# A conv-mixer trunk layer on one core: the written order kept on every engine through the first loop, x normed as it lands, tiny loads on GpSimd's queue

## The chip, the core and the metric

The kernel runs on one core of a Trainium2 chip. Five engines work side by side, each on a queue of its own and in order: TensorE (PE; PEld is its weight load), VectorE (DVE), ScalarE (ACT), GpSimd (POOL) and SyncE (SP), which only issues DMA transfers here. They wait for each other by semaphores. The metric is the device time of one execution in microseconds (us); lower is better.

## The reference, cut to what matters

One layer is computed. c is the conditioning vector; x has 2048 rows of 1024 float32 numbers.

```
def short_conv_mixer(h, w_in, conv_w, conv_b, w_out):
    u, gc, gb, z = jnp.split(h @ w_in, 4, axis=-1)
    v = gc * u
    conv = ...   # causal, depthwise, width 3, over the sequence
    y = gb * (conv + conv_b) * jax.nn.silu(z)
    return y @ w_out

    shift, scale, gate = ada_modulation(c, ada_w, ada_b)   # silu(c) @ w + b, split in three
    h = rmsnorm(x) * (1.0 + scale) + shift
    x = x + gate * short_conv_mixer(h, ...)
    return rmsnorm(x, final_g)
```

## The kernel before, in words

The sequence is cut into two halves of 1024 rows and each half into two blocks of 512. The four quarters of w_in (8192 columns) are taken in pairs g of 2 x 128 columns. For each pair a 2x2 scheme of seven products (Strassen's, in Winograd's form) stands for the eight block products, so a pair needs seven calls of `product`, 12 matmuls each. Every operand is split into a high part, rounded by ScalarE (`nc.scalar.copy`), and a low part, subtracted by VectorE (`tensor_sub`); three passes low-high, high-high and high-low make one float32 product.

Until its end the first loop is another matter, and it is what is changed. It runs over the eight slices k of 128 features of x. In step k TensorE multiplies slice k of h with the early weights of six pairs: 18 matmuls (line L542 before, L590 after) into six banks `ps["A"]`. Between these matmuls it does the steps of small jobs, one step after each matmul: `turn_h0(k + 1)` transposes the next slice of the four normed tiles of x0 (L143), has ScalarE make h from it (`make_h`, L147), splits it into b, and splits the early weights we of that slice; `turn_h1` does the same for the second block from k = 4 on, two slices in a step; `turn_mod(k + 2)` finishes the modulation (shift and scale) of a slice by small matmuls (L195).

The modulation of two slices is summed mostly on VectorE: `sum_mod` adds the scaled tiles of ada_w into the tile `mod` (L184, six instructions, four for the first), which starts with ada_b in its first row. The rest of the sum is done by the matmuls of `turn_mod`, of which the last for each of shift and scale reads `mod`. After step 3 the six banks hold the product P1, which is kept by copies (L359), three on VectorE and three on ScalarE; step 4 goes on in the same banks.

The norm of x (`norm_x`) is a square with a sum on ScalarE (L110), two GpSimd instructions on one column for 1/sqrt (ms L116, rs L118) and a scaling on VectorE (L133). `make_conv` loads the conv parameters and transposes them on TensorE (L243) into cpar. `warm_up(n)` is n matmuls on ones whose result is not used.

After the loop the 32 pairs of products follow (L300). `prepare(n)` loads the weights of product n if they are not there and splits its operand w; it runs four products ahead. `make_t3` and `make_t4` (L556, L561) make sums of h that the first of these products need later.

Buffers come from pools: raw has four (512 KB, early weights, weights, and in before the scratch of the squares too), op has 33, w has 6, PSUM has 8 banks, of which six are the early ones. The order on each engine is chosen by a scheduler that works on the recorded instructions with their dependencies and the order of writing as priority; loads wait in SyncE's queue in their order, and each also for the semaphore of the load eight before it.

Of the kernel before, what the change touches and what calls it, by code (L numbers as in the profile page):

```python
# [8 lines left out]
F32 = mybir.dt.float32  # L9
# [4 lines left out]
P = 128  # L14
# [4 lines left out]
def trunk_kernel(ctx: ExitStack, tc: tile.TileContext, x, c, final_g, ada_w, ada_b,  # L19
# [20 lines left out]
    nc = tc.nc  # L40
    S, D = x.shape
    E = w_out.shape[0]
    CW = conv_w.shape[0]
# [23 lines left out]
    def raw(name="raw"):  # L67
        return rawp.tile([P, D], F32, name=name, tag="raw")
# [32 lines left out]
    def warm_up(ps, a, n):  # L101

        for _ in range(n):
            nc.tensor.matmul(ps[:, :a.shape[1]], lhsT=a[:, :P], rhs=a, start=True, stop=True)


    def square_sum(src, scratch):

# [12 lines left out]
    def load_x(ci):  # L121

        xs = []
        for t in range(ci * ST, (ci + 1) * ST):
            a = op("xn", F32)
            nc.sync.dma_start(a.rearrange("p h n -> p (h n)"), x[t * P:(t + 1) * P, :])
            xs.append(a)
        return xs

    def norm_x(a):  # L130

        scratch = raw("sq").rearrange("p (h n) -> p h n", h=2)
        nc.vector.tensor_scalar_mul(a, a, rstd(square_sum(a, scratch)))  # L133

    def turn_x(xns, k):
# [27 lines left out]
    def mod_start(k):  # L163

        m = sp.tile([P, 2, MC], F32, name="mod", tag="sp")
        nc.gpsimd.memset(m, 0.0)
        nc.sync.dma_start(m[0:1], ada_b.rearrange("(o t n) -> o t n", o=1, t=3)[:, 0:2, k * P:k * P + MC])
        return m

    def load_ada(k):  # L170

        tiles = []
        for r in range(0, KD, AR):
            a = op("ada", F32).rearrange("p r (t n) -> p r t n", t=2)
            for t in range(2):
                nc.sync.dma_start(a[:, :, t, :], ada_v[:, r:r + AR, t, k * P:k * P + MC])
            tiles.append(a)
        return tiles
# [52 lines left out]
    def make_conv():  # L231

        rs = []
        for h in range(E // D):
            r = op("conv", F32).rearrange("p h n -> p (h n)")
            cols = slice(h * D, (h + 1) * D)
            nc.sync.dma_start(r[0:CW, :], conv_w[:, cols])
            nc.sync.dma_start(r[CW:CW + 1, :], conv_b[cols].unsqueeze(0))
            rs.append(r)
        ps = bank()  # L240
        for j in range(NJ):
            i = j % KD
            nc.tensor.transpose(ps[:, j * (CW + 1):(j + 1) * (CW + 1)], rs[j // KD][:CW + 1, i * P:(i + 1) * P],  # L243
                                ident[:CW + 1, :CW + 1])
        nc.vector.tensor_copy(cpar.rearrange("p j w -> p (j w)"), ps[:, :NJ * (CW + 1)])
# [166 lines left out]
    EU = 3  # L412
# [4 lines left out]
    def load_early(k):  # L417
        r = raw()[:, :2 * EU * P]
        for i, q in enumerate((Z, GC)):
            nc.sync.dma_start(r[:, i * EU * P:(i + 1) * EU * P].rearrange("p (j n) -> p j n", j=EU),  # L420
                              w_view[:, k, q, 0:EU, :])
        return r
# [27 lines left out]
    def sum_mod(k):  # L450
        mod_sum(mods[k], ada[k][:ON_DVE.get(k, KD // AR - 1)])

    def turn_mod(k):
        k2 = k // 2 * 2
        yield from mod_turn(mods[k2], ada[k2][ON_DVE.get(k2, KD // AR - 1):], k)

    def turn_h0(k):

        tp = bank()
        for t in range(ST):  # L460
            turn_one(tp, x0, k, t)
            if t < ST - 1:
                yield
        if k % KH == 0:
            h0.extend(half_block())
        make_h(h0[k], tp, k)
        bops[1 if k < KH else 2].append(split_op(h0[k]))
        split_early(k)
        yield
# [20 lines left out]
    def run_all(job):  # L490
        for _ in job:
            pass

    warm_up(early[-1].ps["A"], ones, 28)
    x0 = load_x(0)
    make_conv()
    for k in range(0, KD, 2):
        mods[k] = mod_start(k)
    ada[0] = load_ada(0)
    for k in range(2):  # L500
        we[k] = load_early(k)
    ada[2] = load_ada(2)
    for k in range(2, 4):
        we[k] = load_early(k)
    for a in x0:
        norm_x(a)
    sum_mod(0)
    warm_up(early[-1].ps["A"], ones, 16)
    for k in range(2):
        run_all(turn_mod(k))  # L510
    run_all(turn_h0(0))
    warm_up(early[-1].ps["A"], ones, 8)
    sum_mod(2)
    x1 = None
    for k in range(KD):
        if k == 0:
            ada[4] = load_ada(4)
            x1 = load_x(1)
            we[4] = load_early(4)
        elif k == 1:  # L520
            we[5] = load_early(5)
            ada[6] = load_ada(6)
        elif k == 2:
            we[6] = load_early(6)
            we[7] = load_early(7)
        jobs = []
        if k + 1 < KD:
            jobs.append(turn_h0(k + 1))
        if k >= KH:
            jobs += [turn_h1(2 * (k - KH) + i) for i in range(2)]  # L530
        if k + 2 < KD:
            jobs.append(turn_mod(k + 2))
        b = bops[1 if k < KH else 2][k % KH]
        if k == 1:
            sum_mod(4)
        if k == 3:
            for a in x1:
                norm_x(a)
            sum_mod(6)
        for n, (i, m) in enumerate(PASSES):  # L540
            for e, pr in enumerate(early):
                nc.tensor.matmul(pr.ps["A"], lhsT=wk[k][i][:, e * P:(e + 1) * P], rhs=b[:, m],  # L542
                                 start=k == 0 and n == 0, stop=k % KH == KH - 1 and n == 2, skip_group_check=True)
                while jobs and next(jobs[0], StopIteration) is StopIteration:
                    jobs.pop(0)
        for j in jobs:
            run_all(j)
        if k == KH - 1:
            for e, pr in enumerate(early):
                pr.keep_p1(kept(e, "p1"), nc.scalar.copy if e % 2 else nc.vector.tensor_copy)  # L550
    for e, pr in enumerate(early):
        pr.take_c11(kept(e, "c11"))

    def make_t3():
        for k in range(KH):
# [72 lines left out]
            yield  # L628


    work = [(0, g + d, p) for g in range(0, 2 * EU, 2) for p in (6, 5, 7, 4, 3) for d in range(2)]
    work += [(0, g, p) for g in range(2 * EU, NG) for p in ORDER]
    work += [(1, g, p) for g in range(NG) for p in ORDER]
    pairs = {(0, pr.g): pr for pr in early}
    weights, ready = {}, {}
    AHEAD = 4

    def prepare(n):
        if n >= len(work):
            return  # L640
        hf, g, p = work[n]
        for d in (0, 1):
            i = (hf * NG + g + d)
            if i < 2 * NG and i not in weights:
                weights[i] = Weights(i % NG)
        ready[n] = weights[hf * NG + g].operand(p)

    def side():
        yield from make_second()
        yield from make_gate()  # L650

    jobs = []
    for n in range(AHEAD):
        prepare(n)
    make_t3()
    second = {}
# [124 lines left out]
```

## Time and profile before

| | us |
|---|---|
| median of 3 runs | 1658.1 (1656.35 to 1658.23) |
| the profiled execution | 1657.11 |
| its span in the trace | 1655.3 |
| TensorE busy in it | 1624.2 (98%) |
| VectorE busy | 1036.7 (63%) |
| ScalarE busy | 532.6 (32%) |
| GpSimd busy | 163.7 (10%) |

The profile is of one execution. Its span ends with the last instruction; the execution's own time is 1.8 us longer. Shares of busy time are means over stages that have different limits.

### The profile page before, as it was taken

What the parts mean: (1) busy time and instruction counts of PE and PEld (TensorE: products, weight loads), DVE (VectorE), ACT (ScalarE), POOL (GpSimd) and SP (SyncE); (2) the same over time, 40 slices, a digit from 0 to 9 for tenths busy, and PEclk for the clock granted to TensorE, in tenths of its full rate; (3) what the DMA queues carried; (4) which work ended last, traced back from release to release, by engine and by line L of the source; (5) the groups of instructions that cost most, each with busy time, mean ns of one, the idle gap of its engine ahead of it and who ended that gap; (6) DMA issues with size and microseconds to landing.
All of it is one profiled execution on the core that took longest, in us unless ns stands there. A gap on an engine that the chain in (4) does not pass through costs nothing.

```text
span 1655.3 us, 19334 instructions
## 1 busy us (share of the span) xinstructions
PE 1624.2 (98%) x7276; PEld 1341.6 (81%) x7276; DVE 1036.7 (63%) x1596; ACT 532.6 (32%) x889; POOL 163.7 (10%) x234
## 2 busy tenths in 40 slices
PE   6999999999999999999999999999999999999997
PEld 6778788888888878888888888888888888888886
DVE  3798776777878876666666666666666742223331
ACT  2563344444433333333333333333333520111110
POOL 2101111101111110000001000111000100000000
PEclk7999999999999999999999999999999999999999
DMA  7624324244535632932222222222224633333320
GB/s 231 202 76 121 108 90 140 87 156 166 189 96 181 203 108 76 365 94 77 64 64 64 66 79 73 71 64 70 66 84 118 216 114 102 102 102 102 102 89 26
DMA packets 213103, 190.58 MB, mean 115 GB/s; under 512 B 7425, under 2 KB 181513, under 8 KB 213010
## 3 DMA queue, kind: packets, MB, share of 16 engines
q1 hardware_dynamic: 213010, 189.35, 36.1%
q8 instruction: 57, 0.93, 0.2%
q14 instruction: 36, 0.29, 0.1%
HBM read 144.75 MB, written 44.56 MB: 114 GB/s over the span
## 4 chain that ended last, share of the span: by engine, by line
PE 71%; issue 18%; DVE 6%; DMA 3%; POOL 2%; SPq 0%; ACT 0%; POOLq 0%; DVEq 0%; ACTq 0%
PE ps L300 63%; PE ps L718 5%; DMA raw<-in_l_w_in_dram 2%; DVE w L151 1%; PE ps L542 1%; POOL rs L118 1%; DMA ada<-in_l_ada_w_dram 1%; PE ps L143 1%; DVE b L151 1%; POOL t L323 1%; POOL ms L116 0%; DVE gate_m L216 0%; DVE t L322 0%; DVE raw L282 0%; DVE s L285 0%
## 5 line engine op out<-in xcount | busy, mean ns | idle before, releaser
L300 PE MATMUL ps<-b,w 128*128 128x512 f32 x5232 | 1192.5, 390 | 5.9 <-DVE v L387 2.4
L300 PEld LDWEIGHTS ps<-b,w 128*128 128x128 f32 x5232 | 980.4, 188 | 211.1 <-DVE v L387 3.3
L150 ACT CAST w<-raw 128x512 fp32r<-128x512 f32 x244 | 151.6, 623 | 371.4 <-PE ps L300 289.6
L150 ACT CAST w<-s 128x512 fp32r<-128x512 f32 x192 | 118.5, 618 | 202.2 <-PE ps L300 178.1
L718 PE MATMUL ps<-wo,ye 128*128 128x512 f32 x768 | 180.5, 394 | 0.0
L718 PE MATMUL ps<-wo,yw 128*128 128x512 f32 x768 | 176.8, 389 | 0.0
L151 DVE TENSOR_TENSOR w<-s,w 128x512 fp32r<-128x512 f32 x192 | 131.7, 687 | 67.9 <-ACT w L150 67.5
L718 PEld LDWEIGHTS ps<-wo,ye 128*128 128x128 f32 x768 | 144.2, 188 | 33.8
L151 DVE TENSOR_TENSOR w<-raw,w 128x512 fp32r<-128x512 f32 x244 | 168.3, 690 | 4.8 <-ACT w L150 4.6
L718 PEld LDWEIGHTS ps<-wo,yw 128*128 128x128 f32 x768 | 144.1, 188 | 30.3
L731 DVE TENSOR_TENSOR a<-ps,gate 128x512 f32<-128x512 f32 x32 | 22.0, 691 | 192.3 <-PE ps L718 192.2
L322 DVE SCALAR_TENSOR_TENSOR t<-v,cpar,t 128x512 f32<-128x512 f32 x128 | 95.8, 749 | 39.1 <-ACT t L320 38.3
L110 ACT ACTIVATE sq<-xa 128x1024 f32<-128x1024 f32 x16 | 17.0, 1060 | 274.2 <-DVE xa L732 251.7
L318 POOL COPY v<-v 128x2 f32<-128x2 f32 x32 | 21.4, 667 | 648.6 <-DVE v L370 618.5
L324 DVE TENSOR_TENSOR t<-t,gb 128x512 f32<-128x512 f32 x64 | 44.3, 692 | 53.9 <-POOL t L323 53.9
L275 DVE TENSOR_TENSOR s<-raw 128x512 f32<-128x512 f32 x64 | 44.1, 689 | 48.0 <-DMA raw<-in_l_w_in_dram 47.9
L399 DVE TENSOR_TENSOR u<-ps,u 128x512 f32<-128x512 f32 x58 | 40.0, 689 | 40.0 <-PE ps L300 40.0
L359 ACT COPY u<-ps 128x512 f32<-128x512 f32 x58 | 34.0, 586 | 91.4 <-PE ps L300 85.8
L320 ACT ACTIVATE t<-v,cpar 128x512 f32<-128x512 f32 x64 | 52.0, 814 | 5.1 <-DVE v L406 4.7
L116 POOL TENSOR_SCALAR ms<-ss 128x1 f32<-128x1 f32 x32 | 11.8, 369 | 411.5 <-ACT sq L110 387.1
L323 POOL TENSOR_TENSOR t<-t,sz 128x512 f32<-128x512 f32 x29 | 40.2, 1387 | 114.4 <-DVE t L322 94.1
L542 PE MATMUL ps<-b,we 128*128 128x512 f32 x144 | 46.9, 448 | 4.4 <-ACT b L150 1.5
(95 smaller groups left out, 998.6 us busy)
## 6 DMA issues: line engine op xcount, KB each, us to landing
raw<-in_l_w_in_dram SPq DMA_DIRECT2D x128, 512.0 KB
y_d<-t SPq DMA_DIRECT2D x64, 256.0 KB
yr<-y_d SPq DMA_DIRECT2D x32, 512.0 KB
op_d<-b SPq DMA_DIRECT2D x28, 512.0 KB
b<-op_d SPq DMA_DIRECT2D x28, 512.0 KB
xn<-in_x_dram SPq DMA_DIRECT2D x16, 512.0 KB
ada<-in_l_ada_w_dram SPq DMA_DIRECT2D x32, 256.0 KB
raw<-in_l_w_out_dram SPq DMA_DIRECT2D x16, 512.0 KB
```

Of the source, the lines that this page charges most:

```text
L150: nc.scalar.copy(hi, src)
L151: eng.tensor_sub(lo, src, hi.bitcast(F32))
L275: nc.vector.tensor_add(d, a21, a22)
L300: nc.tensor.matmul(ps, lhsT=w[:, i, k * P:(k + 1) * P], rhs=b[k][:, m], start=first and k == 0 and n == 0, stop=k == KH - 1 and n == 2, sk ...
L320: nc.scalar.activation(t, v[:, 2:], AF.Identity, bias=cpar[:, j, 3:4], scale=cpar[:, j, 2:3])
L322: nc.vector.scalar_tensor_tensor(t, v[:, w:CH + w], cpar[:, j, w:w + 1], t, ALU.mult, ALU.add)
L323: nc.gpsimd.tensor_mul(t, t, self.sz[ci])
L324: nc.vector.tensor_mul(t, t, self.gb[ci])
L359: (eng or nc.scalar.copy)(a, self.ps["A"])
L399: nc.vector.tensor_add(self.u, ps, self.u)
L542: nc.tensor.matmul(pr.ps["A"], lhsT=wk[k][i][:, e * P:(e + 1) * P], rhs=b[:, m], start=k == 0 and n == 0, stop=k % KH == KH - 1 and n == 2 ...
L718: nc.tensor.matmul(ps, lhsT=a, rhs=b, start=j == 0 and n == 0, stop=j == NJ - 1 and n == 2)
```

## The change

Five things are done. A helper `in_order` ties every instruction that is recorded between `mark` and the end of the first loop to the one before it on the same engine, so that the scheduler keeps the written order there. The code of that part is written in another order to go with it: the norm of x0 and `make_conv` stand before the modulation; the first slice's transposes before its modulation's sums; `sum_mod(4)`, `norm_all(x1)` and `sum_mod(6)` are jobs that stand behind `turn_h0` in steps 1 and 3; the first two `prepare` stand in the last step; the number of warm-ups is 28, 12, 16 and 4 in place of 28, 16 and 8. The scratch of `norm_x` comes from the pool op in place of raw. The loads of ada_b (four) and of the conv parameters (four) are issued by GpSimd in place of SyncE. The loads of ada slice 4 and of the first weights are issued earlier in the code.

```
+    def in_order(mark):
+
+        last = {}
+        for i in nc.cur_bb.bb.instructions[mark:]:
+            if i.engine in last:
+                tc.add_manual_dep(i, last[i.engine].name, mybir.DependencyInfo(
+                    mybir.DependencyClass.NoSync, mybir.DependencyReason.DATA), reason="in_order")
+            last[i.engine] = i
...
-        scratch = raw("sq").rearrange("p (h n) -> p h n", h=2)
+        scratch = op("sq", F32)
...
-        nc.sync.dma_start(m[0:1], ada_b.rearrange("(o t n) -> o t n", o=1, t=3)[:, 0:2, k * P:k * P + MC])
+        nc.gpsimd.dma_start(m[0:1], ada_b.rearrange("(o t n) -> o t n", o=1, t=3)[:, 0:2, k * P:k * P + MC])
...
-            nc.sync.dma_start(r[0:CW, :], conv_w[:, cols])
-            nc.sync.dma_start(r[CW:CW + 1, :], conv_b[cols].unsqueeze(0))
+            nc.gpsimd.dma_start(r[0:CW, :], conv_w[:, cols])
+            nc.gpsimd.dma_start(r[CW:CW + 1, :], conv_b[cols].unsqueeze(0))
...
+    def load_weights(i):
+        if i < 2 * NG and i not in weights:
+            weights[i] = Weights(i % NG)
...
+    def now(f, *args):
+
+        f(*args)
+        return
+        yield
+
+    def norm_all(xs):
+        for a in xs:
+            norm_x(a)
+
+    mark = len(nc.cur_bb.bb.instructions)
     warm_up(early[-1].ps["A"], ones, 28)
     x0 = load_x(0)
+    begin()
+    norm_all(x0)
     make_conv()
...
-    for a in x0:
-        norm_x(a)
+    warm_up(early[-1].ps["A"], ones, 12)
+    first = turn_h0(0)
+    for _ in range(ST - 1):
+        next(first)
     sum_mod(0)
     warm_up(early[-1].ps["A"], ones, 16)
-    for k in range(2):
-        run_all(turn_mod(k))
-    run_all(turn_h0(0))
-    warm_up(early[-1].ps["A"], ones, 8)
+    run_all(turn_mod(0))
+    run_all(first)
+    warm_up(early[-1].ps["A"], ones, 4)
+    run_all(turn_mod(1))
     sum_mod(2)
...
+            jobs.append(now(sum_mod, 4))
...
+        elif k == 3:
+            load_weights(0)
+            jobs += [now(norm_all, x1), now(sum_mod, 6)]
+        elif k == 5:
+            load_weights(1)
         if k >= KH:
             jobs += [turn_h1(2 * (k - KH) + i) for i in range(2)]
+        if k == KD - 1:
+            jobs += [now(prepare, 0), now(prepare, 1)]
...
-        if k == 1:
-            sum_mod(4)
-        if k == 3:
-            for a in x1:
-                norm_x(a)
-            sum_mod(6)
...
         pr.take_c11(kept(e, "c11"))
+    in_order(mark)
...
-    for n in range(AHEAD):
+    for n in range(2, AHEAD):
         prepare(n)
```

`begin` holds the loads that stood between `make_conv` and the norm of x0 before, and those of ada slice 4. How the rows move shows at three places. Line numbers are 9 higher in the new kernel at first, 48 higher in the loop.

The first is the start of the program. On TensorE it began so, L243 being the transposes of the conv parameters and L195 `turn_mod`:

```order
L104 MATMUL ps<-ones 128x128 x44
L243 MATMUL ps<-ident,conv 128x4 x8
L104 MATMUL ps<-ones 128x128 x8
L243 MATMUL ps<-ident,conv 128x4 x8
L195 MATMUL ps<-sc,ada 128x1 x6
L195 MATMUL ps<-ones,mod 128x1
L195 MATMUL ps<-sc,ada 128x1 x4
L195 MATMUL ps<-ones,mod 128x1
```

It now begins with fewer warm-ups, then all conv transposes, and three transposes of x (L152) stand between the warm-ups that follow:

```order
L104 MATMUL ps<-ones 128x128 x28
L252 MATMUL ps<-ident,conv 128x4 x16
L104 MATMUL ps<-ones 128x128 x12
L152 MATMUL ps<-ident,xn 128x128 x3
L104 MATMUL ps<-ones 128x128 x16
L204 MATMUL ps<-sc,ada 128x1 x4
L204 MATMUL ps<-ones,mod 128x1
L204 MATMUL ps<-sc,ada 128x1 x4
L204 MATMUL ps<-ones,mod 128x1
```

The loads that those conv transposes wait for are now on GpSimd, where they stand behind the last of the four norms of x0 (ms and rs of its fourth tile are the first two rows):

```order
L125 TENSOR_SCALAR ms<-ss 128x1
L127 TENSOR_TENSOR rs<-ms,nhalf 128x1
L246 DMA conv<-in_l_conv_w_dram 3x1024
L247 DMA conv<-in_l_conv_b_dram 1x16x64
L246 DMA conv<-in_l_conv_w_dram 3x1024
L247 DMA conv<-in_l_conv_b_dram 1x16x64
```

In before they were the first loads of SyncE's queue behind the four of x.

The second place is the end of step 3 on VectorE, where the norm of x1 (xn), the sums of the last modulation (mod) and the copies of P1 (keep) stand. Before, the scheduler had mixed them among the splits b and we:

```order
L151 TENSOR_TENSOR b<-hr,b 128x512 x2
L184 SCALAR_TENSOR_TENSOR mod<-ada,sc,mod 128x512
L133 TENSOR_SCALAR xn<-xn,rs 128x1024
L184 SCALAR_TENSOR_TENSOR mod<-ada,sc,mod 128x512
L133 TENSOR_SCALAR xn<-xn,rs 128x1024
L151 TENSOR_TENSOR b<-hr,b 128x512
L133 TENSOR_SCALAR xn<-xn,rs 128x1024
L151 TENSOR_TENSOR we<-raw,we 128x768
L133 TENSOR_SCALAR xn<-xn,rs 128x1024
L359 COPY keep<-ps 128x512 x3
L151 TENSOR_TENSOR we<-raw,we 128x768
```

Now all of the norm and of the sums stands ahead of the copies, and the splits of steps 3 and 4 around them:

```order
L160 TENSOR_TENSOR b<-hr,b 128x512
L160 TENSOR_TENSOR we<-raw,we 128x768
L142 TENSOR_SCALAR xn<-xn,rs 128x1024 x4
L193 SCALAR_TENSOR_TENSOR mod<-ada,sc,mod 128x512 x6
L368 COPY keep<-ps 128x512 x3
L160 TENSOR_TENSOR b<-hr,b 128x512
L160 TENSOR_TENSOR we<-raw,we 128x768
```

The third place is the end of the loop on VectorE. The names t hold the last four sums of the second block, s the sums of the first weights, w the operands of the first products. Before, the operands w were split among the last sums:

```order
L151 TENSOR_TENSOR b<-hr,b 128x512
L151 TENSOR_TENSOR w<-s_836,w 128x512
L486 TENSOR_TENSOR t_737<-hr 128x512
L151 TENSOR_TENSOR w<-s_823,w 128x512
L486 TENSOR_TENSOR t_752<-hr 128x512
L151 TENSOR_TENSOR b<-t_737,b 128x512
L151 TENSOR_TENSOR w<-s_834,w 128x512
L151 TENSOR_TENSOR b<-t_752,b 128x512
L486 TENSOR_TENSOR t_773<-hr 128x512
L556 TENSOR_TENSOR hr<-hr 128x512
L486 TENSOR_TENSOR t_788<-hr 128x512
L151 TENSOR_TENSOR b<-t_773,b 128x512
```

Now the last sum with all that is made from it stands first (L605 and L610 are `make_t3` and `make_t4`), and the first operand w behind it:

```order
L495 TENSOR_TENSOR t_804<-hr 128x512
L605 TENSOR_TENSOR hr<-hr 128x512
L610 TENSOR_TENSOR hr<-hr,t_804 128x512
L160 TENSOR_TENSOR b<-t_804,b 128x512
L284 TENSOR_TENSOR s_811<-raw 128x512
L288 TENSOR_TENSOR s_813<-s_811,raw 128x512
L291 TENSOR_TENSOR raw<-raw 128x512
L160 TENSOR_TENSOR w<-s_813,w 128x512
```

## Rows read from the trace of the kernel before

**Rows 1.** page, busy time of TensorE, share of the span, instructions

```profile
PE 1624.2 (98%) x7276; PEld 1341.6 (81%) x7276; DVE 1036.7 (63%) x1596; ACT 532.6 (32%) x889; POOL 163.7 (10%) x234
```

**Rows 2.** TensorE grouped by line, 92 us to the end; idle before them

```profile
L300 PE MATMUL ps<-b,w 128*128 128x512 f32 x5232 | 1192.5, 390 | 5.9 <-DVE v L387 2.4 <-ACT w L150 1.7 <-DVE gb L385 1.7
```

**Rows 3.** timeline of TensorE, 0 to 135 us (start, length; idle before in brackets)

```profile
15.27 0.66 PE L243 MATMUL ps<-ident,conv 4*128 4x4 f32 x8
17.24 1.02 PE L195 MATMUL ps<-sc,ada 128*128 128x1 f32 x8 [1.31 <-DMA ada<-in_l_ada_w_dram]
18.63 1.01 PE L195 MATMUL ps<-sc,ada 128*128 128x1 f32 x4 [0.37 <-DMA ada<-in_l_ada_w_dram]
...
38.32 0.79 PE L542 MATMUL ps<-b,we 128*128 128x512 f32 x1 [1.52 <-ACT b L150]
```

**Rows 4.** timeline of ScalarE, 0 to 110 us

```profile
2.37 0.21 ACT L81 ACTIVATE sc<-c_sb 128x8 f32<-128x8 f32 x1 [0.36 <-DMA c_sb<-in_c_dram]
...
27.63 1.06 ACT L110 ACTIVATE sq<-xn 128x1024 f32<-128x1024 f32 x1 [0.29 <-DVE we L151]
...
57.85 1.06 ACT L110 ACTIVATE sq<-xn 128x1024 f32<-128x1024 f32 x1 [3.22 <-issue]
```

**Rows 5.** timeline of SyncE's queue (length is the issue, not the transfer)

```profile
0.72 0.39 SPq L79 DMA_DIRECT2D c_sb<-in_c_dram  x1
...
3.96 0.26 SPq L237 DMA_DIRECT2D conv<-in_l_conv_w_dram  x1
...
5.10 4.84 SPq L167 DMA_DIRECT2D mod<-in_l_ada_b_dram  x4
9.99 4.98 SPq L176 DMA_DIRECT2D ada<-in_l_ada_w_dram  x8
```

**Rows 6.** timeline of GpSimd, 0 to 100 us

```profile
1.66 1.45 POOL L166 MEMSET mod<- 128x512 f32 x3
28.87 0.34 POOL L116 TENSOR_SCALAR ms<-ss 128x1 f32<-128x1 f32 x1 [25.75 <-ACT sq L110]
...
32.45 1.32 POOL L118 TENSOR_TENSOR rs<-ms,nhalf 128x1 f32<-128x1 f32 x1
...
34.56 0.93 POOL L118 TENSOR_TENSOR rs<-ms,nhalf 128x1 f32<-128x1 f32 x1
```

**Rows 7.** windows: busy us by engine, granted clock, DMA share, GB/s

```profile
0.00:8.00 8.00, 6.96 (x47) 6.96 (x48) 0.65 (x4) 1.49 (x2) 2.55 (x10) 1.00 0.72 259
...
18.00:19.00 1.00, 0.63 (x5) 0.55 (x4) 0.96 (x2) 0.00 (x0) 0.00 (x0) 0.59 1.11 365
...
42.00:43.00 1.00, 1.00 (x7) 0.92 (x8) 0.82 (x2) 0.65 (x2) 0.00 (x0) 0.97 0.87 262
```

**Rows 8.** ScalarE, then VectorE: timeline rows of the operations of a loop step

```profile
36.84 0.78 ACT L147 ACTIVATE hr<-ps,shift,scale 128x512 f32<-128x512 f32 x1 [4.22 <-PE ps L143]
37.65 0.62 ACT L150 CAST b<-hr 128x512 fp32r<-128x512 f32 x1
...
42.41 0.83 ACT L150 CAST we<-raw 128x768 fp32r<-128x768 f32 x1 [0.35 <-DMA ada<-in_l_ada_w_dram]
...
28.38 4.68 DVE L184 SCALAR_TENSOR_TENSOR mod<-ada,sc,mod 128x512 f32<-128x512 f32 x6
...
35.52 0.75 DVE L133 TENSOR_SCALAR xn<-xn,rs 128x1024 f32<-128x1024 f32 x1 [0.46 <-POOL rs L118]
36.18 0.95 DVE L151 TENSOR_TENSOR we<-raw,we 128x768 fp32r<-128x768 f32 x1
38.30 0.69 DVE L151 TENSOR_TENSOR b<-hr,b 128x512 fp32r<-128x512 f32 x1 [1.16 <-ACT b L150]
...
67.20 1.88 DVE L359 COPY keep<-ps 128x512 f32<-128x512 f32 x3
```

**Rows 9.** timeline of TensorE again: step k = 4, and the first main product

```profile
67.94 0.50 PE L542 MATMUL ps<-b,we 128*128 128x512 f32 x1 [1.37 <-DVE keep L359]
...
92.18 16.48 PE L300 MATMUL ps<-b,w 128*128 128x512 f32 x72
```

More of the change, by code (lines that the diff above doesn't have):

```diff
@@ L492, in run_all, with prepare, begin @@
             pass
+    work = [(0, g + d, p) for g in range(0, 2 * EU, 2) for p in (6, 5, 7, 4, 3) for d in range(2)]
+    work += [(0, g, p) for g in range(2 * EU, NG) for p in ORDER]
+    work += [(1, g, p) for g in range(NG) for p in ORDER]
+    pairs = {(0, pr.g): pr for pr in early}
+    weights, ready = {}, {}
+    AHEAD = 4
+    def load_weights(i):
+        if i < 2 * NG and i not in weights:
+            weights[i] = Weights(i % NG)
+    def prepare(n):
+        if n >= len(work):
+            return
+        hf, g, p = work[n]
+        for d in (0, 1):
+            load_weights(hf * NG + g + d)
+        ready[n] = weights[hf * NG + g].operand(p)
+    def begin():
+        for k in range(0, KD, 2):
+            mods[k] = mod_start(k)
+        ada[0] = load_ada(0)
+        for k in range(2):
+            we[k] = load_early(k)
+        ada[2] = load_ada(2)
+        for k in range(2, 4):
+            we[k] = load_early(k)
+        ada[4] = load_ada(4)
+    def now(f, *args):
+        f(*args)
+        return
+        yield
[3 more added lines that the diff above has]
+    mark = len(nc.cur_bb.bb.instructions)
     warm_up(early[-1].ps["A"], ones, 28)
     x0 = load_x(0)
+    begin()
+    norm_all(x0)
     make_conv()
-    for k in range(0, KD, 2):
-        mods[k] = mod_start(k)
-    ada[0] = load_ada(0)
-    for k in range(2):
[L501 to L504, printed above, removed]
-    for a in x0:
-        norm_x(a)
+    warm_up(early[-1].ps["A"], ones, 12)
+    first = turn_h0(0)
+    for _ in range(ST - 1):
+        next(first)
     sum_mod(0)
     warm_up(early[-1].ps["A"], ones, 16)
-    for k in range(2):
-        run_all(turn_mod(k))
-    run_all(turn_h0(0))
-    warm_up(early[-1].ps["A"], ones, 8)
+    run_all(turn_mod(0))
+    run_all(first)
+    warm_up(early[-1].ps["A"], ones, 4)
+    run_all(turn_mod(1))
     sum_mod(2)
-    x1 = None
     for k in range(KD):
+        jobs = []
+        if k + 1 < KD:
+            jobs.append(turn_h0(k + 1))
         if k == 0:
-            ada[4] = load_ada(4)
             x1 = load_x(1)
@@ L525, in trunk_kernel @@
             we[7] = load_early(7)
-        jobs = []
-        if k + 1 < KD:
-            jobs.append(turn_h0(k + 1))
+        elif k == 3:
[3 more added lines that the diff above has]
+            load_weights(1)
         if k >= KH:
             jobs += [turn_h1(2 * (k - KH) + i) for i in range(2)]
+        if k == KD - 1:
+            jobs += [now(prepare, 0), now(prepare, 1)]
         if k + 2 < KD:
@@ L628, in begin_out @@
             yield
[L631 to L646, printed above, removed]
     def side():
```

## The prediction

> **What bounds the kernel now.** I read the summary page first. TensorE is busy 98% of the span [rows 1], so a change can win only where TensorE stands still, or where something pushes that standing still further out. The grouping of TensorE's instructions from 92 us to the end leaves 5.9 us of idle time in front of all 5,232 main products [rows 2]. Everything else that can be won lies in the first 92 us, the part that this change reorders. Both ends of that part stand in the TensorE timeline: the first loop matmul starts at 38.32 [rows 3], step k = 4 at 67.94 and the first main product at 92.18 [rows 9]. From there on TensorE runs almost without a gap, so a microsecond by which the first main product moves is about a microsecond of the result.
>
> Why is the first matmul so late? On ScalarE the first square of x waits for VectorE's split of an early weight and starts at 27.63 [rows 4], because the scratch of the squares is a buffer of the four-deep raw ring, which the early weights hold. Yet the first tile of x had landed by 5.10: there SyncE's next load, which waits for its semaphore, goes out [rows 5].
>
> The sum runs against the profiled execution's own 1657.1 us, 1.8 us over its span and 1.0 us below the median of the runs. I take 0.2% (3.3 us) as the least that a measurement of this kernel tells from no change.
>
> **Part 1, the start.** With scratch of its own, the norm of x0 follows the loads. GpSimd, though, now issues eight DMAs, and the four conv loads stand behind its last rstd. Three memsets end at 3.11 today [rows 6]; the four modulation loads between them add 4d, where d is one issue on GpSimd, which no row shows. The nearest rows: SyncE issues such a load in as little as 0.26 [rows 5]; GpSimd needs 0.93 to 1.32 for a power on one column, which is all overhead [rows 6]. I take 1.0, since it is software on that engine, and keep 0.26 and 1.3 as ends. The first square can reach GpSimd at 5.10 + 1.24 (27.63 to 28.87 [rows 4, 6]) = 6.3, so with d = 1.0 the memsets and issues end later, at 7.1. The four ms/rs pairs took 28.87 to 35.49, 6.6 us [rows 6]: 13.7. The last conv load is issued 3 d later, at 16.7. Its landing: 1.65 us on an empty queue (c_sb, issue at 0.72, used at 2.37 [rows 4, 5]); about 4.1 us behind bulk loads (the last of the eight ada issues, near 14.5, is used at 18.6 [rows 3, 5]). The queue is full here, so I take the middle, 2.9: the conv tables are in at 19.6.
>
> On this point the Trainium skill speaks against the change: "DMA: Bandwidth & Descriptors", section "Anatomy of one DMA — SWDGE (gpsimd) path", gives a DMA issued from GpSimd a fixed cost of about 2.0 us. By that figure, as an estimate, the landing would come 0.9 us sooner and the sum below would be 0.9 us smaller; no run here shows it yet.
>
> What stands behind them on TensorE, in order: the conv transposes (0.66 [rows 3]), 12 warm-ups, three transposes of x, 16 warm-ups, turn_mod(0). TensorE has then been idle since about 9 us. The granted clock fell to half (0.59 in that slice) about 2.7 us after the last dense work at 15.9 [rows 3, 7], so these 28 warm-ups start at 1.2 GHz. At the program's start 47 records, two a warm-up, took from 1.04 to 8.0 [rows 7], so 28 take about 8.0. The transposes take 0.5. Turn_mod(0) has 20 records at 1.02 / 8 [rows 3]: 2.5. Then the shift and last transpose 0.5, ScalarE's make_h 0.78, cast of b 0.62, cast of we 0.83, VectorE's we 0.95 [rows 8]: 3.7. Sum 15.4; first loop matmul at 19.6 + 15.4 = 35.0, against 38.3: **−3.3 us**. With the low ends (d 0.26, landing 1.65) it is 30.8, −7.5; with the high ones (1.3, 4.1) 38.3, no gain.
>
> SyncE's queue gets shorter and the bulk loads land some 3 us earlier. I price that at nothing: in the new order the loop waits for VectorE and TensorE, and the loads are hidden behind them.
>
> **Part 2, steps k = 0 to 3.** A step without waits is 24.24 / 4 = 6.1 (67.94 to 92.18 [rows 9]). In k = 0, turn_mod(2) ends in a matmul on mod[2], whose six sums now stand behind the split of we[0]: 4.68 [rows 8], while TensorE gets there after 7 of 18 matmuls, 2.4: a wait of 2.3.
>
> In k = 3 norm_all and sum_mod(6) are queued on VectorE ahead of the three copies that keep P1, and step 4's first matmul overwrites the bank of the first copy. From the step's first matmul: four matmuls with the transposes 1.4; make_h, b, we 2.23 [rows 8]; first square to GpSimd 1.24; four ms/rs pairs 6.6; the last xn 0.75; six sums 4.68; one copy 0.63 (three in 1.88 [rows 8]). Sum 17.6, of which TensorE has work for 6.1. Today the same squares start at 57.85 [rows 4] in the scheduler's order, ten microseconds ahead of step 4, and the copies cost only 1.37 [rows 9]. In the new order nothing covers the chain. Steps 0 to 3 take 3 × 6.1 + 2.3 + 17.6 = 38.2, against 29.6 (38.32 to 67.94): **+8.6 us**.
>
> **Part 3, k = 4 to the first main product.** ScalarE serves in order, and each h1 tile now holds it for make_h 0.78, VectorE's subtraction 0.69 and its cast 0.62. A step costs ScalarE 2.23 + 2 × 2.09 = 6.4. From 1.4 after the start, three steps and step 7's two tiles: 1.4 + 19.2 + 4.2 = 24.8. Then VectorE, in the written order: two subtractions and a b (2.1), S1 and S2 (1.4), ScalarE's cast 0.62, the split of w 0.69: 29.6, and about 0.9 because VectorE has four operations a tile (2.8) against the 2.09. So 30.5 against 24.24: **+6.3 us**, most of it a gap of some 6 us ahead of the first product, where prepare(0) now stands last.
>
> **Part 4, what follows gaps.** After two such gaps (11 and 6 us) I expect half clock, as after 15.9. The loop's first matmul took 0.79 and the full clock came back by 42.1 [rows 3, 7], 3.7 us after 38.3, so each costs up to 1.8: **+3 us**, as part of it lies in waits (ends 0 and 3.7). In the main loop the second operand is split about 1 us late, and of the 5.9 us of idle [rows 2] about half should vanish, as VectorE stands further ahead of TensorE when that starts: **−2 us** (ends −5 and +1).
>
> Sum: −3.3 + 8.6 + 6.3 + 3 − 2 = +12.6; 1657.1 + 12.6 = 1669.7 us.
>
> **Rivals.**
> - *Even.* The order holds, but every open price falls on its good end: conv in early (−7.5 for −3.3), no drop of the clock (0 for 3), the idle time back (−5 for −2): 12.6 − 4.2 − 3 − 3 = +2.4, 1659.5. For it: GpSimd has nothing else to do there. Against it: three independent goods at once.
> - *Faster.* The start decides: if GpSimd hands its loads to the queue without holding them behind its own work, conv lands with the last tile of x, near 9.4 (the fourth modulation load, which waits for that tile, is out at 9.94 [rows 5]). The first matmul would then stand at 9.4 + 15.4 = 24.8, a gain of 13.5; with 8.6 + 6.3 against it and part 4 at its best end, −5, the sum is −3.6: 1653.5. It decides once that first matmul comes before about 25. Against it: the conv loads stand behind four rs, which themselves wait for the last tile of x.
> - *Much slower.* Each issue costs GpSimd 2 us or more, or both turn_mods run at half clock (2.5 more for each): the first matmul at 40 to 45, the sum 1675 to 1680. For it: GpSimd's rows are long. Against it: a cheap SyncE issue.
>
> **How the numbers follow.** Forecast 62%, even 14%, faster 9%, much slower 15%. The range 1657 to 1680 leaves out the faster case and the upper half of the last, under 2 in 10. Slower by over 0.2%: 0.62 + 0.15 = 0.77; within: 0.14; faster: 0.09.
>
> **What the new profile would show.** Right: conv transposes near 19 to 20, first loop matmul near 35, a TensorE gap of about 11 us before step 4 that ends with VectorE's copy, a second gap of about 6 us before the first main product, the first product near 104. Wrong: a first matmul before 25; the squares of x1 well before step 3's copies are due; or products that follow the loop without a gap. If the gaps are there and the time is not, the 5.9 us of later idle came back in full.

## The result and the profile after

The changed kernel takes 1675.8 us in the median (1671.7 to 1681.1, 4 runs) against 1658.2 (1656.4 to 1664.0, 4 runs) for the kernel before on the same chip: a ratio of 1.0106, 95% interval 1.009 to 1.0122. The profiled execution took 1675.6 us with a span of 1673.8, so 18.5 us of span were added.

TensorE's instructions grouped by line and tile (busy us, mean ns of one, idle us in front of them with what ended it) answer to [rows 2]:

```profile
L309 PE MATMUL ps<-b,w 128*128 128x512 f32 x5232 | 1197.1, 391 | 11.7 <-DVE w L160 6.9 <-DVE v L396 2.7 <-DVE gb L394 1.2
...
L590 PE MATMUL ps<-b,we 128*128 128x512 f32 x144 | 53.6, 487 | 10.6 <-DVE keep L368 10.4 <-DVE we L160 0.2
...
L252 PE MATMUL ps<-ident,conv 4*128 4x4 f32 x16 | 2.0, 242 | 8.5 <-DMA conv<-in_l_conv_b_dram 8.5
```

Three waits stand out: 8.5 us for the conv tables, 10.4 for a copy of P1, and 6.5 of the 6.9 in front of the first main product. The start, on GpSimd's timeline and then on TensorE's:

```profile
11.47 0.57 POOL L127 TENSOR_TENSOR rs<-ms,nhalf 128x1 f32<-128x1 f32 x1
11.99 0.93 POOL L246 DMA_DIRECT2D conv<-in_l_conv_w_dram  x1
12.92 0.53 POOL L247 DMA_DIRECT2D conv<-in_l_conv_b_dram  x1
...
13.94 0.51 POOL L247 DMA_DIRECT2D conv<-in_l_conv_b_dram  x1
```

```profile
18.25 0.98 PE L252 MATMUL ps<-ident,conv 4*128 4x4 f32 x8 [7.91 <-DMA conv<-in_l_conv_b_dram]
19.85 0.98 PE L252 MATMUL ps<-ident,conv 4*128 4x4 f32 x8 [0.61 <-DMA conv<-in_l_conv_b_dram]
20.76 4.46 PE L104 MATMUL ps<-ones 128*128 128x128 f32 x24
...
34.76 0.79 PE L590 MATMUL ps<-b,we 128*128 128x512 f32 x1 [0.23 <-DVE we L160]
```

x is normed with the loads (the last rs at 11.47), the tables' last load goes out at 13.94 and is used at 19.85, and the first loop matmul stands at 34.76 instead of 38.32 [rows 3]. VectorE's timeline ahead of step 4 and ahead of the first main product:

```profile
67.87 0.75 DVE L142 TENSOR_SCALAR xn<-xn,rs 128x1024 f32<-128x1024 f32 x1 [0.76 <-POOL rs L127]
68.54 4.68 DVE L193 SCALAR_TENSOR_TENSOR mod<-ada,sc,mod 128x512 f32<-128x512 f32 x6
73.14 1.88 DVE L368 COPY keep<-ps 128x512 f32<-128x512 f32 x3
...
103.90 0.68 DVE L160 TENSOR_TENSOR b<-t,b 128x512 fp32r<-128x512 f32 x1
...
106.59 0.69 DVE L160 TENSOR_TENSOR w<-s,w 128x512 fp32r<-128x512 f32 x1
```

And TensorE's main products up to the first transposes of x's second half (243.66 us; before, these stood at 225.12):

```profile
107.34 19.11 PE L309 MATMUL ps<-b,w 128*128 128x512 f32 x72 [6.48 <-DVE w L160]
126.84 27.53 PE L309 MATMUL ps<-b,w 128*128 128x512 f32 x120 [0.39 <-DVE w L160]
156.40 29.10 PE L309 MATMUL ps<-b,w 128*128 128x512 f32 x120 [2.03 <-DVE v L396]
186.21 57.61 PE L309 MATMUL ps<-b,w 128*128 128x512 f32 x252 [0.71 <-DVE v L396]
```

The first 72 records took 19.11 us, not 16.48 [rows 9], and the granted clock is what differs: 0.50 from 108 to 112 us. In the view by windows the columns are the stretch, its length, busy us (and records) of TensorE, its weight loads, VectorE, ScalarE and GpSimd, then the granted clock, the DMA share and GB/s:

```profile
18.00:22.00 4.00, 3.13 (x22) 3.09 (x23) 1.10 (x3) 0.00 (x0) 0.00 (x0) 0.50 1.10 348
...
34.00:36.00 2.00, 1.77 (x8) 1.33 (x9) 1.96 (x3) 0.23 (x2) 0.00 (x0) 0.55 0.93 355
...
42.00:45.00 3.00, 3.00 (x10) 2.32 (x9) 0.00 (x0) 0.00 (x0) 0.00 (x0) 0.59 0.81 226
...
74.00:78.00 4.00, 4.00 (x13) 2.91 (x13) 1.02 (x2) 1.00 (x2) 0.00 (x0) 0.50 0.00 0
...
108.00:112.00 4.00, 4.00 (x11) 3.13 (x10) 3.08 (x5) 2.88 (x6) 0.00 (x0) 0.50 0.46 131
...
156.00:160.00 4.00, 3.60 (x10) 2.86 (x11) 4.00 (x8) 1.09 (x2) 0.00 (x0) 0.64 0.02 8
```

The 18.5 us add up: first loop matmul 34.76 − 38.32 = −3.6; steps 0 to 3, 39.2 against 29.6, +9.6; step 4 to the first product, 33.4 against 24.2, +9.1; from there to the side transposes, 136.3 against 132.9, +3.4.

### The profile page after: what moved, and what is told of

It reads as the page before. It is cut to its first block, busy times and chain, and to the rows that moved or that the text cites. A ratio compares the mean times of both kernels' runs of the same rounds, so it can differ in the third digit from the quotient of the medians.

```text
span 1673.8 us, 19386 instructions
## 1 busy us (share of the span) xinstructions
PE 1631.9 (97%) x7292; PEld 1347.8 (81%) x7292; DVE 1037.0 (62%) x1596; ACT 533.1 (32%) x889; POOL 163.1 (10%) x242
## 4 chain that ended last, share of the span: by engine, by line
PE 72%; issue 19%; DVE 4%; DMA 2%; POOL 2%; ACT 1%; SPq 0%; POOLq 0%; DVEq 0%; ACTq 0%
PE ps L309 65%; PE ps L750 5%; DMA raw<-in_l_w_in_dram 1%; PE ps L590 1%; PE ps L152 1%; DVE w L160 1%; POOL rs L127 1%; POOL t L332 0%; DMA xn<-in_x_dram 0%; DVE gate_m L225 0%; ACT b L159 0%; POOL ms L125 0%; DVE b L160 0%; DVE raw L291 0%; DVE mod L193 0%
## 5 line engine op out<-in xcount | busy, mean ns | idle before, releaser
L590 PE MATMUL ps<-b,we 128*128 128x512 f32 x144 | 53.6, 487 | 10.6 <-DVE keep L368 10.4
L332 POOL TENSOR_TENSOR t<-t,u 128x512 f32<-128x512 f32 x29 | 39.4, 1357 | 117.8 <-issue 79.2
```

The source lines that it names most:

```text
L332: nc.gpsimd.tensor_mul(t, t, self.sz[ci])
```

## The experiments

The theory was that the order loses at two places, ahead of step 4 and ahead of the first product, and that half clock behind each gap adds to it. The rivals: the moved loads and the scratch cost the time; or the work of VectorE and ScalarE behind step 3 is the limit, and any gap that is closed comes back. All runs are read by three points of TensorE's timeline: F, the first loop matmul; S, the start of step 4; T, the first transposes of x's second half (the side transposes). From T to the end of the span every kernel takes 1428.6 to 1430.2 us.

S is step 4's first matmul, with two exceptions. In the three kernels in the scheduler's order (before, no order, and no order with conv late) one matmul of step 4 stands ahead of the wait for VectorE's copy, and S is the one behind that wait. In the kernel before this first one stands at 66.09, S at 67.94 [rows 9]:

```profile
66.09 0.48 PE L542 MATMUL ps<-b,we 128*128 128x512 f32 x1
```

Counted alike, F to S would be 0.5 us shorter and S to T 0.5 us longer in these three. In x1 early and six moves S is step 4's second matmul, 0.3 us behind the first. Ratios are against the kernel before on the same chip, with their 95% interval. A row of the table is one execution; that of prepare first is 6.6 us faster than its median, four moves 2.6 and h1 in pairs 3.0 faster, t held back 4.5 slower.

| kernel | F | S | T | F to S | S to T | span |
|---|---|---|---|---|---|---|
| before | 38.32 | 67.94 | 225.12 | 29.6 | 157.2 | 1655.3 |
| changed | 34.76 | 73.97 | 243.66 | 39.2 | 169.7 | 1673.8 |
| no order | 47.76 | 80.63 | 237.00 | 32.9 | 156.4 | 1666.3 |
| x1 early | 35.03 | 65.04 | 230.92 | 30.0 | 165.9 | 1660.3 |
| prepare first | 37.59 | 74.48 | 243.37 | 36.9 | 168.9 | 1672.0 |
| conv late | 23.52 | 61.62 | 231.69 | 38.1 | 170.1 | 1661.6 |
| h1 in pairs | 34.49 | 77.59 | 246.64 | 43.1 | 169.1 | 1675.2 |
| warm gap | 37.51 | 83.00 | 249.24 | 45.5 | 166.2 | 1678.4 |
| four moves | 23.52 | 56.21 | 225.99 | 32.7 | 169.8 | 1654.7 |
| t held back | 37.62 | 80.64 | 251.24 | 43.0 | 170.6 | 1681.3 |
| copies on ScalarE | 37.59 | 72.72 | 242.30 | 35.1 | 169.6 | 1671.0 |
| six moves | 23.53 | 51.99 | 221.16 | 28.5 | 169.2 | 1651.3 |
| no order, conv late | 42.82 | 71.34 | 227.42 | 28.5 | 156.1 | 1656.7 |

**No order.**

```diff
-    in_order(mark)
```

> The changed kernel with the written order taken off again: the scheduler may move instructions as before, the loads on GpSimd, the scratch and the new place of each call stay. Theory (the fixed order pays for itself at two places, ahead of step 4 and ahead of the first main product): both gaps, 10.4 and 6.5 us in the changed kernel's trace, shrink to a few microseconds, the first product comes near 93 instead of 107.3, and the time is 1656 to 1663 us. Rival (the moved loads and the scratch cost the time, whatever the order): 1671 us or more.

1667.8 us, 1.0054 (1.0038 to 1.0071): between the two. Both gaps are gone (the largest wait left in front of step 4 is 1.53), but the start is worse. TensorE's timeline:

```profile
36.69 0.98 PE L252 MATMUL ps<-ident,conv 4*128 4x4 f32 x8 [19.26 <-DMA conv<-in_l_conv_b_dram]
...
47.76 0.80 PE L590 MATMUL ps<-b,we 128*128 128x512 f32 x1 [0.83 <-ACT b L159]
```

So the theory is right behind F, where the order costs 208.9 − 189.2 = 19.7 us up to T. The rival is right at the start: the conv loads stand behind GpSimd's rs, which in the scheduler's order are late again, and the tables come at 36.7. In the changed kernel F stands 13 us earlier, and that hid part of what the order costs behind it.

**x1 early.**

```diff
         if k == 0:
...
+            jobs.append(now(norm_all, x1))
         elif k == 1:
...
         elif k == 2:
...
+            jobs.append(now(sum_mod, 6))
         elif k == 3:
             load_weights(0)
-            jobs += [now(norm_all, x1), now(sum_mod, 6)]
```

> The changed kernel with the order still fixed, but x1's norm written in step 0 and the last six sums in step 2, both in places where VectorE stands idle in its trace (41 to 47.6 us and 55.3 to 60.5 us). Theory (the three copies that step 4 waits for stand behind that chain): the gap of 10.4 us ahead of step 4 falls to about 1.4, step 4 starts near 65 instead of 74.0, and the time falls by 9 to 11 us (11 if the half clock behind the gap goes as well). Rival (VectorE's and ScalarE's work of steps 4 to 7 is the bound, so the gap only moves): the gap ahead of the first product grows by what the first one loses, and the time falls by less than 3 us.

1663.1 us, 1.0033 (1.0022 to 1.0044), 12.7 under the changed kernel's median, a little more than the theory's 9 to 11, and the two intervals are apart. Step 4 starts without a wait, and the second gap is as it was:

```profile
65.04 0.48 PE L591 MATMUL ps<-b,we 128*128 128x512 f32 x1
...
96.22 4.11 PE L309 MATMUL ps<-b,w 128*128 128x512 f32 x10 [6.46 <-DVE w L160]
```

The first gap is that chain, and it did not move into the second one.

**Prepare first.**

```diff
+        if k == KD - 1:
+            jobs.append(now(prepare, 0))
         if k >= KH:
             jobs += [turn_h1(2 * (k - KH) + i) for i in range(2)]
         if k == KD - 1:
-            jobs += [now(prepare, 0), now(prepare, 1)]
+            jobs.append(now(prepare, 1))
```

> The changed kernel with the first main product's weight operand (two sums, a cast, a split) written ahead of step 7's two tiles of h1, not behind them. Theory (that operand is the last thing the first product waits for): VectorE uses 1.4 us in which it is idle, the product starts with its first 512 columns ready and follows the tiles, and the time falls by 3 to 5 us. Rival (the tiles of h1 themselves end last, and the product waits for the last of them): under 1 us.

1.0123 (1.0102 to 1.0144): no gain. The wait is only cut in pieces, 1.76 and three of 0.3 to 0.8 us in the first product and 3.28 ahead of the second, whose operand is now the late one; they add up to the 6.5 of the changed kernel:

```profile
102.69 2.06 PE L309 MATMUL ps<-b,w 128*128 128x512 f32 x8 [1.76 <-DVE w L160]
...
111.26 19.11 PE L309 MATMUL ps<-b,w 128*128 128x512 f32 x74 [3.28 <-DVE w L160]
```

**Conv late.** `make_conv` is cut in two: `load_conv` issues the loads where `make_conv` stood, and `make_conv(conv)`, the transposes and the copy, is a job of step 1.

```diff
-    make_conv()
+    conv = load_conv()
...
         elif k == 1:
...
-            jobs.append(now(sum_mod, 4))
+            jobs += [now(sum_mod, 4), now(make_conv, conv)]
```

> The changed kernel with the conv tables' transposes and copy written in step 1; their loads stay where they are on GpSimd. Theory (the tables' landing, 18.25 and 19.85 us, sets the start, as warm-ups, transposes and VectorE's first sums all stand behind it): the first loop matmul comes near 27 instead of 34.8 and the time falls by 5 to 8 us. Rival (the weights and modulation tiles that the loop needs land no earlier, so the loop waits for loads instead): the first matmul comes early, but the time falls by less than 3 us.

1663.5 us, 1.0036 (1.0027 to 1.0046). F is 11.2 us earlier, more than the theory's 8, and all of it arrives. The loads did not become the limit.

**Scratch alone, in the kernel before.**

```diff
-        scratch = raw("sq").rearrange("p (h n) -> p h n", h=2)
+        scratch = op("sq", F32)
```

> The kernel before with one line of the change alone: the squares' scratch is a buffer of the op pool, not of the raw ring. The scheduler's order and the loads on SyncE stay. Theory (the wait of the first square for VectorE's split of an early weight, 27.63 us, sets the start): x is normed soon after the first weights land, near 20 us, the first loop matmul comes near 30 instead of 38.3, and the time falls by 5 to 8 us, 1650 to 1653. Rival (the modulation's tiles and VectorE's sums set the start anyway): the first loop matmul stays above 36 and the time within 2 us of before.

1655.4 us, 0.998 (0.9971 to 0.9989), a little faster, but not by this theory. ScalarE's timeline shows that the squares still start at 28.05. They no longer wait for a buffer, but stand behind the first modulation's copies, for which ScalarE waits 22.5 us, and two casts:

```profile
25.20 0.16 ACT L198 COPY shift<-ps 128x1 f32<-128x1 f32 x1 [22.53 <-PE ps L195]
...
26.60 1.56 ACT L150 CAST we<-raw 128x768 fp32r<-128x768 f32 x2
28.05 1.07 ACT L110 ACTIVATE sq<-xn 128x1024 f32<-128x1024 f32 x1
```

F is 39.49, no earlier than before, and T is 225.05 against 225.12. The buffer was only the first of two things in front of the squares; the scheduler's order is the other, so what the prediction says of the square at 27.63 us names one cause of two. Of the 1.4 us by which its span is shorter than before 1.3 lie behind T, within the 1.6 us by which the kernels differ there, so where the gain comes from is not shown.

**h1 in pairs**: in each step both `make_h` of h1 stand ahead of the subtractions and splits, which are now in `split_h1`.

```diff
...
         make_h(h1[k], tp, k)
+        if k % 2 == 0:
+            return
+        yield
+        split_h1(k - 1)
+        split_h1(k)
...
```

> The changed kernel with the tiles of h1 taken in pairs: both make_h of a step are written ahead of the subtractions and splits, so that ScalarE no longer stands between a tile's make_h and its cast until VectorE has subtracted (0.95 to 1.11 us a tile in the changed kernel's trace). Theory (that standing, eight times, is what makes the tiles late at the loop's end): the gap of 6.5 us ahead of the first product shrinks by 2 to 4 us and so does the time. Rival (VectorE, with four operations a tile at 0.6 us each and no idle time from 92 us on, is what is late): under 1 us.

1.0122 (1.0107 to 1.0137), and the gap is 6.49: the rival. On VectorE the last tiles stand without idle time, four operations each, 2.4 us from split to split:

```profile
100.00 0.68 DVE L160 TENSOR_TENSOR b<-t,b 128x512 fp32r<-128x512 f32 x1
100.60 0.68 DVE L504 TENSOR_TENSOR t<-hr 128x512 f32<-128x512 f32 x1
101.20 1.28 DVE L618 TENSOR_TENSOR hr<-hr,t 128x512 f32<-128x512 f32 x2
102.41 0.68 DVE L160 TENSOR_TENSOR b<-t,b 128x512 fp32r<-128x512 f32 x1
```

**Warm gap.**

```diff
...
                 pr.keep_p1(kept(e, "p1"), nc.scalar.copy if e % 2 else nc.vector.tensor_copy)
+            warm_up(bank(), ones, 60)
```

> The changed kernel with 60 warm-up matmuls of 128 columns written on TensorE between step 3 and step 4, where it stands idle for 10.4 us; their result is used by nobody. Theory (behind the gap TensorE runs at the low clock, granted 0.50 from 74 to 78 us, and that is lost time on its own): step 4's first matmul takes 0.48 instead of 0.77 us, and the time falls by 1.5 to 3 us. Rival (ScalarE and VectorE set the pace of steps 4 to 7, so a faster TensorE there gains nothing): under 1 us.

1.0118 (1.0103 to 1.0134). The filling was too long, 13.3 us for a gap of 10.4. But the clock held:

```profile
69.68 13.56 PE L104 MATMUL ps<-ones 128*128 128x128 f32 x120
83.00 0.48 PE L590 MATMUL ps<-b,we 128*128 128x512 f32 x1
```

From S to the first product (114.52) it takes 31.5 us instead of 33.4, so the half clock behind this gap costs 1.9 us, as the theory has it. Of the 3.5 us by which S to T is shorter the rest lies in the products, where the slow stretch at 156 us did not come. The gain does not show in the time: F came 2.8 us later, the filling is 2.9 us too long, and steps 0 to 3 took 3.4 us more, with the granted clock at 0.50 up to 50 us. So the time alone decides nothing.

**Four moves**: conv late, x1's norm in step 2, h1 in pairs, `prepare(0)` in step 6.

> The changed kernel with four moves at once, all still in a fixed order: the conv tables turned in step 1, x1's norm written in step 2 (in step 0 it would stand before x1 lands), the tiles of h1 in pairs, and the first product's weight operand written at the start of step 6. Theory (the start, the gap ahead of step 4 and the gap ahead of the first product are three separate losses that add): -11 at the start, -5 ahead of step 4, -4 ahead of the first product, so 1651 to 1657 us, faster than the kernel before. Rival (with an early start the loads, 350 GB/s up to 44 us, or VectorE are the next bound, and the gains do not add): 1659 us or more.

1659.1 us, 1.0004 (0.9992 to 1.0016): even, nearer to the rival. The start and F to S gain as expected, and S to T stays at 169.8. The 6.5 us ahead of the first product are gone, but step 7 now waits 1.62 us for ScalarE, the first product 1.6 in three pieces, and the second 3.28 for its operand.

**t held back**: the subtractions of `make_t3` and `make_t4` depend on the fixed part's last VectorE instruction; `behind` makes that tie.

```diff
-    make_t3()
+    behind(last, make_t3)
...
-            make_t4()
+            behind(last, make_t4)
```

> The changed kernel with the eight subtractions of make_t3 and make_t4, which come after the fixed part and which the scheduler puts between the last four tiles of h1, held behind it on VectorE. Theory (VectorE's four operations a tile, 2.41 us, are what is late ahead of the first product): a tile takes ScalarE's 2.09 us again, the last split of t2 ends 1 to 2 us earlier from the loop's last step, the gap of 6.5 us falls to about 5 and the time by 1 to 2 us. Rival (the four tiles in a row on ScalarE and VectorE are late by themselves, whatever stands between them): gap and time stay within 0.5 us.

1.013 (1.0115 to 1.0145). The gap falls as the theory says, and S to T does not, because the wait returns ahead of the second product (0.39 there in the changed kernel):

```profile
112.19 18.09 PE L319 MATMUL ps<-b,w 128*128 128x512 f32 x72 [5.03 <-DVE w L170]
134.12 29.86 PE L319 MATMUL ps<-b,w 128*128 128x512 f32 x120 [3.84 <-DVE w L170]
```

**Copies on ScalarE.**

```diff
-                pr.keep_p1(kept(e, "p1"), nc.scalar.copy if e % 2 else nc.vector.tensor_copy)
+                pr.keep_p1(kept(e, "p1"), nc.scalar.copy)
```

> The changed kernel with the six copies that keep P1 all on ScalarE; x1's norm and the last six sums stay where the change put them. Theory (step 4's first matmul waits only because its bank's copy is queued on VectorE behind that chain): the gap of 10.4 us in front of step 4 falls to about 2; part of the chain is waited for later, as the first tile of h1 needs the normed x1 and turn_mod(6) the sums, so the time falls by 4 to 7 us. Rival (what step 4 needs is the chain itself, and the copy only happens to be its end): the waits come back in step 4, and the time falls by less than 1.5 us.

1671.7 us, 1.0078 (1.0063 to 1.0094). The wait in front of step 4 falls from 10.4 to 2.5, and 1.28 comes back in step 5:

```profile
72.72 0.50 PE L590 MATMUL ps<-b,we 128*128 128x512 f32 x1 [2.50 <-ACT keep L368]
...
83.35 0.33 PE L152 MATMUL ps<-ident,xn 128*128 128x128 f32 x1 [1.28 <-ACT hr L156]
```

Against the changed kernel's median that is 4.1 us, the theory's lower end, though the two intervals overlap a little (1.009 to 1.0094). The trace is clearer: against the kernel with t held back, whose steps 0 and 1 were as slow, F to S is 7.9 us shorter. So most of the wait in front of step 4 was for a place in a queue, not for the chain's result.

**Six moves**: the four, with the copies on ScalarE and the subtractions held back.

> The kernel with four moves at once (conv tables turned in step 1, x1's norm in step 2, tiles of h1 in pairs, first weight operand in step 6) and two more: the six copies of P1 on ScalarE, and the subtractions of make_t3 and make_t4 held behind the fixed part. Theory (its two gaps left, 5.0 us ahead of step 4 and 3.3 us ahead of the second product, have these two causes): -3 to -4 and -1 to -3, so 1651 to 1655 us. Rival (the six copies make ScalarE late, 3 us in step 4, and the waits only move): 1658 us or more.

1652.7 us, 0.9971 (0.9955 to 0.9988): faster than the kernel before, and the time is as the theory has it. Its second half is not borne out: against four moves F to S is 4.2 us shorter, S to T only 0.6, where 1 to 3 were expected. F is 14.8 us earlier than in the kernel before and T only 4.0: S to T is still 169.2, its waits now in the products.

```profile
85.43 15.46 PE L323 MATMUL ps<-b,w 128*128 128x512 f32 x60 [2.85 <-DVE w L170]
103.49 28.98 PE L323 MATMUL ps<-b,w 128*128 128x512 f32 x120 [2.60 <-DVE w L170]
```

**No order, conv late**: the edits of no order and of conv late together.

> The changed kernel with the written order taken off and the conv tables turned in step 1: the two earlier runs that had one of these each came to 1667.8 and 1663.5 us. Theory (the order costs about 20 us behind the first loop matmul and saves about 12 ahead of it; the late conv tables cost about 11 either way): x is again normed only near 35 us, behind VectorE's sums, the first loop matmul comes near 38, the side transposes 189 us later, and the time is 1655 to 1660 us, that of the kernel before. Rival (the loads on GpSimd or the scratch cost time by themselves inside the loop): 1663 us or more.

1659.6 us, 1.0013 (1.0001 to 1.0024), within 0.2% of the kernel before. F is 42.8, not 38, as x is normed late, and F to T is 184.6. So loads on GpSimd and scratch cost nothing that shows inside the loop (F to T was 186.8 before); the rival falls.

## Why the prediction was right, and where its sizes were off

Slower was right, and both gaps are there, near their predicted lengths (10.4 for 11.5, 6.5 for about 6). The time came out 6 us over the forecast, inside the range.

**Part 1** gave −3.3, and it was −3.6, by two errors that cancel. An issue on GpSimd costs 0.51 to 0.93, not 1.0, and the four ms/rs pairs took 5.4 us (6.60 to 12.04), not 6.6, so the last issue stood at 13.94 instead of 16.7; from its start to its use took 5.9 us, not 2.9. As an estimate, the fixed 2.0 us that the Trainium skill's "DMA: Bandwidth & Descriptors", section "Anatomy of one DMA — SWDGE (gpsimd) path", gives would have had the tables in at 15.9; this trace disagrees, at 350 GB/s of other loads. That the sum of this part came out so close is luck. One reading is off without effect: by the 0.59 of the slice from 18 to 19 us [rows 7] the clock of the kernel before fell near 18.2, not 18.6. That the tables set the start is shown by conv late; the faster rival's point of decision, a first matmul before 25, is what that kernel reaches.

**Part 2** gave +8.6 and was +9.6 (+10.1 counted alike, as the prediction too reads 67.94 as step 4's first matmul). The gap's cause, a copy queued on VectorE behind norm and sums, is shown twice, by x1 early and by the copies on ScalarE. The 2.3 us wait in step 0 came as 0.5: the granted clock was 0.55 from 34 to 36 us, and TensorE was late itself. The prediction prices no half clock at this place. So this sum too is close by errors that cancel: its two waits are 2.9 us too long (11.5 and 2.3 for 10.4 and 0.5), and the rest of steps 0 to 3 took 28.3 us, not 4 × 6.1 = 24.4.

**Part 3** gave +6.3 and was +9.1. TensorE's idle time in it is 6.5 us, so the gap was right in size. The other 2.6 us are TensorE's busy time (26.86 against 24.24, in the windows below): 0.5 is the matmul at 66.09, which the window of before leaves out, and 2.1 are clock. What failed is the reason. I had the gap as the end of one chain, with `prepare(0)` last. Three runs that go at this chain in three ways (prepare first, h1 in pairs, t held back) gain at most 0.8 us from S to T. What they point to instead is VectorE's whole work behind S. The windows of the kernel before and of the changed one, from step 4 to the first product:

```profile
67.94:92.18 24.24, 24.24 (x138) 19.83 (x139) 21.09 (x34) 18.13 (x33) 0.00 (x0) 1.00 0.22 64
```

```profile
73.97:107.34 33.37, 26.86 (x140) 21.22 (x141) 23.62 (x37) 17.78 (x30) 0.58 (x1) 0.91 0.16 48
```

VectorE (third busy figure) is the engine to look at. From S to the same place in the products, the start of the row of 252 records (167.87 before, 186.21 after), the two windows are:

```profile
67.94:167.87 99.93, 95.74 (x451) 78.05 (x451) 89.71 (x144) 47.61 (x83) 12.23 (x11) 1.00 0.35 100
```

```profile
73.97:186.21 112.24, 102.60 (x452) 82.53 (x453) 92.77 (x145) 49.22 (x85) 9.10 (x11) 0.93 0.31 89
```

Before, VectorE is busy for 89.7 of 99.9 us (90%) there; after, for 92.8 of 112.2. Of the 12.3 us more, some 9 are idle time of VectorE. In steps 4 to 7 the fixed order leaves it idle for 9.8 us, against 3.2 before. In 2.8 of these a split waits for ScalarE's cast and the cast for the subtraction in front; most of the rest stands at the start of the steps (3.41, 1.96 and 1.39 us), where the cast waits for `make_h` and that for TensorE's transposes. Behind the loop the longest idle time of VectorE up to that place is a wait for a load of weights:

```profile
78.43 0.69 DVE L160 TENSOR_TENSOR b<-hr,b 128x512 fp32r<-128x512 f32 x1 [3.41 <-ACT b L159]
...
151.01 0.69 DVE L284 TENSOR_TENSOR s<-raw 128x512 f32<-128x512 f32 x1 [2.59 <-DMA raw<-in_l_w_in_dram]
```

By this reading, what is not done in time is waited for later, under whatever name is queued last. The ten kernels in a fixed order in the table take 165.9 to 170.6 us from S to T, the three in the scheduler's order 156.1 to 157.2. That VectorE's idle time is the cause is argued from these rows, not shown, and steps 4 to 7 are not all of it: six moves leaves VectorE idle for only 6.4 us from S to the first product and still takes 169.2, with three waits of VectorE for such loads (1.23, 2.53 and 1.67 us) in the products. No run fixed steps 4 to 7 in the scheduler's own order, so it stays open how much of it the tiles' order is and how much the order of the weight operands.

**Part 4** had +3 for the clock and −2 of idle time given back. From S to T TensorE is busy for 160.05 us against 152.99, and 153.47 with the matmul at 66.09: 6.6 us, which I read as clock, since the slow stretches lie there. Behind the first product the waits sum to 3.1 us (0.39, 2.03, 0.71) against 4.2, so 1.1 came back.

The forecast's error of 5.9 us is then the clock from S on, +3.6 (6.6 for 3), part 2, +1.5, the idle time, +0.9, the second gap, +0.2, less 0.3 at the start. The clock is the term that was mis-sized. Two slow stretches were counted, at up to 1.8 us each. From S on there were three: behind the gap ahead of step 4 (2.1 us), in the first product (19.11 for 16.48, 2.6 us) and behind the wait of 2.03 at 156 us (29.10 for 27.53, 1.6 us), together 6.3 of the 6.6. Two more lie in step 0 (0.55 from 34 to 36 us, 0.59 from 42 to 45).

## What to carry to other kernels

Before the order of an engine is fixed by hand, add up that engine's work over the whole stage that follows. Here VectorE was 90% busy behind S, and closing the gap ahead of the first product only moved it, in three runs; the gap ahead of step 4 could be closed for good. Look first for what is queued in front of a small thing that another engine needs (a copy, a table of 64 columns), and move that one thing; here the two such moves, x1's chain and the conv tables, were worth 12 us each. A gap on TensorE is to be priced with the slow stretch behind it: here 1.9 us for one of 10.4.

## What the hardware showed that was not expected

A load that GpSimd issues was used 5.3 to 5.9 us after its issue began (12.92 to 18.25, 13.94 to 19.85), and in the kernel without the order 4.9 us after (31.80 to 36.69), while the DMA engines moved some 350 to 390 GB/s. The issue itself held GpSimd of the changed kernel for 0.5 us, and 0.76 and 0.93 for the first of each four. All eight such loads of the changed kernel landed 4.6 to 5.8 us after their issue, the four of ada_b in the first microseconds too. No run has one without other loads beside it, so whether the time is the queue's or comes with the issuing engine is not shown.

The granted clock also fell where TensorE had no idle time. In the conv-late kernel it was busy all through, ran warm-ups up to 16.4 us and then the modulation's one-column matmuls, with eight records of warm-ups between (18.68 to 19.74):

```profile
16.00:20.00 4.00, 4.00 (x38) 4.00 (x37) 0.00 (x0) 1.22 (x4) 0.00 (x0) 0.97 1.10 333
20.00:23.00 3.00, 3.00 (x16) 3.00 (x15) 2.48 (x4) 1.14 (x2) 0.00 (x0) 0.50 1.10 350
```

So in this kernel the warm-ups ahead of such matmuls did not carry the clock into the loop. How long it then stays low differs between executions of one order: in the profile of the kernel with t held back TensorE ran at 0.50 from 34 to 50 us, all of step 0, and F to S took 43.0 us; the prepare-first kernel, the same up to S, took 36.9. The changed kernel's own four runs spread over 9 us; that this is the reason is likely, not shown.

```profile
34.00:42.00 8.00, 8.00 (x33) 7.08 (x33) 6.08 (x8) 2.54 (x7) 0.00 (x0) 0.50 0.39 143
42.00:50.00 8.00, 8.00 (x26) 6.46 (x25) 1.65 (x2) 1.03 (x4) 0.00 (x0) 0.50 0.61 187
```
